# The factors that join two attention parts: 32 rows sent through DRAM, instead of a spread and 16 transposes on the chip

## The chip, the cores and the metric

The kernel runs on one core of one Trainium2 chip. The time is in device microseconds (us), as the median of several runs of the whole program. A core has a matrix engine (PE, with its weight load shown as PEld), a vector engine (DVE), a scalar engine (ACT), a general engine (POOL), and a queue (SP) that here issues all the transfers (DMAs) between DRAM and the on-chip memory. Each engine, and SP, takes its instructions strictly in order; an instruction that must wait for another engine or for a transfer holds up everything behind it on the same engine.

## The reference

A decoder trunk of two layers, 1024 tokens by 1024 features, in float32. What matters here, cut from the reference:

```python
for l in range(DEPTH):
    h = rmsnorm(x, norm1[l])
    proj = h @ w_in[l]
    qa, ka, va, qb, kb, vb, gate_pre = jnp.split(proj, splits, axis=-1)
    o_a = dilated_mixture(hd4(qa, DSW_HEADS), hd4(ka, DSW_HEADS), hd4(va, DSW_HEADS))
    o_b = stick_breaking_attention(hd4(qb, SB_HEADS), hd4(kb, SB_HEADS), hd4(vb, SB_HEADS))
    g_a, g_b = (sigmoid(gate_pre + b_gate[l]) in two halves)
    merged = g_a * (o_a @ w_br[l, :OUT_A]) + g_b * (o_b @ w_br[l, OUT_A:])
    x = x + merged @ w_o[l]
    h2 = rmsnorm(x, norm2[l])
    ...
# dilated_mixture: three groups of four heads, each with its own window and dilation;
# per head slot the groups' outputs are mixed by their softmax denominators:
alpha = jax.nn.softmax(jnp.stack(lses, axis=0), axis=0)
o = jnp.sum(alpha[..., None] * jnp.stack(outs, axis=0), axis=0)
```

The kernel holds the mixture of the two nearer groups as one unnormalised sum `on` with its own maximum and denominator (`sn`), and the widest group as `ot` with `st1`. Mixing the two needs, for every token and head, two factors: one for `on` and one for `ot`. The features of a head lie on 64 partitions and the tokens run along the free axis, so a factor has to stand in all 64 partitions of its head. The statistics come with the tokens on partitions. Bringing the factors from the one layout to the other is what the change is about.

## The kernel before

Every float32 product is made of three matmuls: both operands are split into a high part and a remainder (ACT casts `w_hi`, `hh`; DVE subtracts to `w_lo`, POOL to `hl`), and high*high, high*low and low*high are summed in PSUM. L182, L183 and L184 are the three matmuls of the plain form (`product`), L1017 to L1019 those of the large input projection.

A layer runs in these stages. The input projection (dense work, L1017 to L1019) is interleaved on PE with attention: a list of attention items is worked off between the dense steps. The last 16 items are the far ones, eight for each of two pairs of heads (`pr` 0 and 1). After the last far item of a pair, `join` mixes `on` and `ot`. `dense.at(n, f)` makes `f` run n dense steps later; the two halves of a join run 2 and 4 steps after the last item.

Then come the branch products, 16 items i = 0 to 15, each a half of the tokens by 128 output features. An item has a product with the attention outputs `oh_a` (called a_i here) and one with `oh_b` (b_i), two times three matmuls each, multiplied by gates `gin` on DVE (L1433), summed into `mrg` (m_i, L1438), and cast and split by ACT (`hh`, L1398) and POOL (`hl`, L1399). The order on PE is b0 b1 b2 a0 a1 a2 a3 b3 a4 b4, and so on to a15 b15. After item i the program loads the gates of item i + 3 (`gate_in`, L1373: 512 KB into one of the four `p4` buffers, which it shares with `fx`), and after i = 1, 5 and 9 the branch weights that items 4, 8 and 12 begin with (`branch_in`, L1391: `br_raw`, 512 KB, split into `br_w` by two ACT casts and two DVE subtractions). The second, third and fourth of these loads in a layer are called br_raw #2, #3 and #4. Then the output projection `o_ps` follows with weights `w_raw`, and the feed-forward part.

PE's order is written out by hand: for the whole program, PE takes its instructions in the order of the code. DVE, ACT, POOL and SP are ordered by a list scheduler, which goes by dependences, priorities and its own estimate of when each is ready. So a change of a few instructions can move others on those four.

The join before, in words: `factors(pr)` computes the two factors as `sf`, a 128 x 16 tile each (L959 to L968, after the last score of the pair). ACT spreads them with four copies (L974) into two tiles `fx`, 64 equal columns a head. The join then makes, for each half, eight transposes of 128 x 128 on PE (L988) into two PSUM banks `j_ps`, and three DVE operations: `jn = ot * j_ps` (L991), `on = on * j_ps` (L992), `on = on + jn` (L993). After them `on` is cast to `oh_a`.

Of the kernel before, what the change touches and what calls it, by code (L numbers as in the profile page):

```python
# [7 lines left out]
F32 = mybir.dt.float32  # L8
# [4 lines left out]
ALU = mybir.AluOpType  # L13
# [3 lines left out]
P = 128  # L17
T = 1024
D = 1024
KD = D // P  # L20
HF = 512
# [12 lines left out]
PT = 6  # L34
# [17 lines left out]
X_AT = (3, 5, 7, 9)  # L52
AHEAD = 200
JOIN = 4


def f32(ap):
# [4 lines left out]
def trunk_kernel(ctx, tc, x, norm1, w_in, b_gate, w_br, w_o, norm2, w_up, conv_w, conv_b, w_down, norm_f, out, depth=None, probe=None):  # L62
    nc = tc.nc
    act, dve, pe, pool = nc.scalar, nc.vector, nc.tensor, nc.gpsimd
# [4 lines left out]
    sb = ctx.enter_context(tc.tile_pool(name="sb", bufs=1))  # L69
    ps = ctx.enter_context(tc.tile_pool(name="ps", bufs=2, space=PSUM))  # L70
    dr = ctx.enter_context(tc.tile_pool(name="dr", bufs=1, space=DRAM))


    ident = cp.tile([P, P], F32, name="ident")
# [46 lines left out]
    sq = [dr.tile([2, 2, 64, T], F32, name=f"sq{i}") for i in range(4)]  # L121
    sv = [dr.tile([P, n, KD, P], F32, name=f"sv{n}") for n in (4, 2, 2)]
    dn = [dr.tile([4, T], F32, name=f"dn{i}") for i in range(2)]

    def bank(tag, name):
        return ps.tile([P, 512], F32, tag=tag, name=name)

    def small(name, dtype=F32):
        return sb.tile([P, 512], dtype, tag="pt", bufs=PT, name=name)
# [431 lines left out]
    R = {}  # L561
# [83 lines left out]
    def scores(o, qt, ql, k):  # L645
        pe.matmul(o, qt, k, start=True, stop=False, skip_group_check=True)
        pe.matmul(o, ql, k, start=False, stop=True, skip_group_check=True)
# [235 lines left out]
    def far_item(dense, pr, s, r, share):  # L883
        i = 8 * pr + 4 * s + r
# [7 lines left out]
        def score():  # L892
            if r == 0:
                bias = share["bias"] = sb.tile([P, 2, 256], F32, tag="bias", name="bias1")
                dve.tensor_scalar(bias[:, 0, :], base0, 4.0 * SLOPES[4 + slot], None, ALU.mult)
                dve.tensor_scalar(bias[:, 1, :], base2, 4.0 * SLOPES[8 + slot], None, ALU.mult)
            bias = share["bias"]
            pt = shared["p"] = sb.tile([P, T], F32, tag="p4", bufs=4, name="p1")
            z0, z1 = bank("s", "z10"), bank("s", "z11")
            t = R["kq", i % 2]  # L900
            for g in range(2):
                scores(z0[:, P * g : P * g + P], t[:, g, 1, 0:P], t[:, g, 2, 0:P], t[:, g, 0, 0:P])
            for g in range(2):
                scores(z1[:, 256 * g : 256 * g + 256], t[:, g, 1, P:256], t[:, g, 2, P:256], t[:, g, 0, :])
            dense.scored = i + 1
            if (s, r) == (1, 0):
                near_stats(pr)
            for n in range(2):
                flat = pt[:, 256:768] if n else pt[:, 0:256]
                if n:  # L910
                    zz, pp, bb = z1, flat, bias.rearrange("p g c -> p (g c)")
                else:
                    zz, pp, bb = z0[:, 0:256].rearrange("p (g c) -> p g c", g=2), flat.rearrange("p (g c) -> p g c", g=2), bias[:, :, P:256]
                nm = st[:, 0, s, n, r : r + 1]
                with tc.high_priority(offset=AHEAD):
                    LAST["red"] = dve.tensor_tensor_reduce(pp, zz, bb, 1.0, 3e38, ALU.add, ALU.min, nm).ins.name
                    act.activation(flat, flat, AF.Exp, bias=nm, scale=-1.0, accum_out=st[:, 1, s, n, r : r + 1])
            if (s, r) == (1, 3):
                factors(pr)

        def turn(g):
            pt = shared["p"]
# [25 lines left out]
    def near_stats(pr):  # L948
        sn = R["sn", pr] = sb.tile([P, 2, 2, 2, 4], F32, tag="sn", bufs=1, name="sn")
        nc.sync.dma_start(sn.rearrange("j a s n r -> j (a s) n r"), tok_view(dn[pr]))  # L950

    def factors(pr):

        sn, st = R["sn", pr], R["st1", pr]
        nat, far_ = (t.rearrange("j a s n r -> j a (s n r)") for t in (sn, st))
        w = sb.tile([P, 6, 16], F32, tag="sw", bufs=1, name="sw")
        f = R["f", pr] = sb.tile([P, 2, 2, 2, 4], F32, tag="sf", bufs=1, name="sf")
        ff = f.rearrange("j a s n r -> j a (s n r)")
        dve.tensor_tensor(w[:, 0, :], nat[:, 0, :], far_[:, 0, :], ALU.min)  # L959
        dve.tensor_tensor(w[:, 1, :], w[:, 0, :], nat[:, 0, :], ALU.subtract)  # L960
        dve.tensor_tensor(w[:, 2, :], w[:, 0, :], far_[:, 0, :], ALU.subtract)
        act.activation(w[:, 1:3, :], w[:, 1:3, :], AF.Exp)
        dve.tensor_tensor(w[:, 3, :], w[:, 1, :], nat[:, 1, :], ALU.mult)
        dve.tensor_tensor(w[:, 4, :], w[:, 2, :], far_[:, 1, :], ALU.mult)
        dve.tensor_tensor(w[:, 3, :], w[:, 3, :], w[:, 4, :], ALU.add)
        dve.reciprocal(w[:, 5, :], w[:, 3, :])
        dve.tensor_tensor(ff[:, 0, :], w[:, 1, :], w[:, 5, :], ALU.mult)
        dve.tensor_tensor(ff[:, 1, :], w[:, 2, :], w[:, 5, :], ALU.mult)  # L968

        R["fx", pr] = []  # L970
        for a in range(2):
            fx = sb.tile([P, 2, 4, 2, 64], F32, tag="p4", bufs=4, name="fx")
            for s in range(2):
                act.copy(fx[:, :, :, s, :], f[:, a, s, :, :].unsqueeze(3).to_broadcast([P, 2, 4, 64]))  # L974
            R["fx", pr].append(fx.rearrange("p n r s c -> p n r (s c)"))

    def join(dense, pr):

        fx, on, ot = R["fx", pr], R["on"], R["ot", pr]
        mine = on[:, pr, :].rearrange("p (n j r) -> p n r j", n=2, r=4)  # L980
        other = ot.rearrange("p (r n j) -> p n r j", r=4, n=2)

        def half_of(n):
            spread = []
            for a in range(2):
                o = bank("to"[a], "j_ps")
                for r in range(4):
                    pe.transpose(o[:, r * P : (r + 1) * P], fx[a][:, n, r, :], ident)  # L988
                spread.append(o.rearrange("p (r j) -> p r j", r=4))
            t = small("jn").rearrange("p (r j) -> p r j", r=4)  # L990
            dve.tensor_tensor(t, other[:, n], spread[1], ALU.mult)  # L991
            dve.tensor_tensor(mine[:, n], mine[:, n], spread[0], ALU.mult)  # L992
            dve.tensor_tensor(mine[:, n], mine[:, n], t, ALU.add)  # L993

        dense.at(2, lambda: half_of(0))
        dense.at(JOIN, lambda: half_of(1))

# [1174 lines left out]
```

## Time and profile before

| | |
|---|---|
| median of 3 runs | 2615.86 us (2615.82 to 2617.07) |
| the profiled execution | 2618.04 us, of which the span from first to last instruction 2616.1 us |
| mean granted TensorE clock | 0.999 |
| PE busy | 2606.0 us (100% of the span) |
| PE weight load, DVE, ACT, POOL busy | 84%, 80%, 52%, 4% |
| chain of work that ended last | PE 96%, everything else 1% or less each |
| DMA | 468.22 MB, mean 179 GB/s, HBM read 303.23 MB and written 162.59 MB |

A matmul row shows a start and a duration. Matmuls overlap: the distance between the starts of two that follow each other is what a matmul takes of PE's time, not the duration in the row. A row with xN is a group of N; a remark in square brackets tells how long the engine stood idle before and what ended that. A DMA row on SP (SPq) shows when the transfer was issued; the time to its landing is given apart.

### The profile page before, as it was taken

Reading aid. Unit: us, or ns where it says so; the run is one execution under the profiler, and the core shown is the slowest. Engines: PE = TensorE matmul, PEld = TensorE weight load, DVE = VectorE, ACT = ScalarE, POOL = GpSimd, SP = SyncE. Lnnn points to the kernel's source line nnn. Section 1 sums busy time; section 2 is a strip of 40 time slices with the busy share of each in tenths; the row PEclk is TensorE's granted clock in tenths of the full one; section 3 lists DMA queues with packets and bytes.
Section 4 is the critical chain, followed back from the end, with each engine's and each line's share of the span. In section 5 each row is a group of like instructions: output and inputs, shape, how many; then the busy total and the mean of one; then the engine's idle time right before and its main releaser. Section 6 shows DMA issues by size and latency. Waiting matters only on the chain.

```text
span 2616.1 us, 36210 instructions
## 1 busy us (share of the span) xinstructions
PE 2606.0 (100%) x12736; PEld 2185.2 (84%) x12736; DVE 2089.5 (80%) x3484; ACT 1357.6 (52%) x2533; POOL 102.2 (4%) x135
## 2 busy tenths in 40 slices
PE   9999999999999999999999999999999999999999
PEld 8888888888888888888888888888888888888888
DVE  7877777795988888897677788777869888889965
ACT  6555666574554555422445555666645555544225
POOL 3000000020000000000000000000300000000000
PEclk9999999999999999999999999999999999999999
DMA  7434578873344444688344436787633344447962
GB/s 254 151 120 132 161 207 217 214 247 93 93 145 153 145 164 142 234 326 317 145 145 147 125 128 180 203 231 210 207 99 119 125 161 146 150 164 260 347 238 111
DMA packets 400418, 468.22 MB, mean 179 GB/s; under 512 B 24308, under 2 KB 315500, under 8 KB 398444
## 3 DMA queue, kind: packets, MB, share of 16 engines
q1 hardware_dynamic: 400220, 465.90, 55.3%
q8 instruction: 101, 1.65, 0.3%
q14 instruction: 81, 0.66, 0.1%
q10 hardware_dynamic: 16, 0.00, 0.0%
HBM read 303.23 MB, written 162.59 MB: 178 GB/s over the span
## 4 chain that ended last, share of the span: by engine, by line
PE 96%; DVE 1%; DMA 1%; ACT 1%; issue 1%; SPq 0%; POOL 0%; DVEq 0%; ACTq 0%
PE u_a L1019 6%; PE u_a L1018 6%; PE u_a L1017 6%; PE d_ps L1780 5%; PE d_ps L1781 5%; PE d_ps L1782 5%; PE i_a L1017 5%; PE i_a L1019 5%; PE i_a L1018 5%; PE u_c L1017 3%; PE u_c L1019 3%; PE u_c L1018 3%; PE i_c L1017 3%; PE i_c L1019 3%; PE i_c L1018 3%; PE o_ps L183 2%
## 5 line engine op out<-in xcount | busy, mean ns | idle before, releaser
L141 ACT CAST w_hi<-up_a 128x512 fp32r<-128x512 f32 x280 | 173.9, 622 | 276.5 <-DVE up_a L1634 120.5
L148 DVE TENSOR_TENSOR w_lo<-up_a,w_hi 128x512 fp32r<-128x512 f32 x280 | 189.3, 688 | 83.6 <-ACT w_hi L141 83.6
L141 ACT CAST w_hi<-in_a 128x512 fp32r<-128x512 f32 x252 | 156.2, 622 | 162.9 <-PE i_c L1018 38.0
L148 DVE TENSOR_TENSOR w_lo<-in_a,w_hi 128x512 fp32r<-128x512 f32 x252 | 172.7, 687 | 75.8 <-ACT w_hi L141 67.0
L1788 DVE TENSOR_TENSOR x<-x,d_ps 128x512 f32<-128x512 f32 (+1 forms) x228 | 153.4, 674 | 65.0 <-PE d_ps L1782 61.6
L1780 PE MATMUL d_ps<-gd_in,w_hi 128*128 128x512 f32 (+1 forms) x340 | 130.0, 382 | 0.0
L1782 PE MATMUL d_ps<-gd_in,w_lo 128*128 128x512 f32 (+1 forms) x340 | 129.8, 382 | 0.0
L1781 PE MATMUL d_ps<-gd_in,w_hi 128*128 128x512 f32 (+1 forms) x340 | 129.7, 382 | 0.0
L1019 PE MATMUL u_a<-hh,w_lo 128*128 128x512 f32 x320 | 124.5, 389 | 0.0
L1018 PE MATMUL u_a<-hl,w_hi 128*128 128x512 f32 x320 | 124.5, 389 | 0.0
L1017 PE MATMUL u_a<-hh,w_hi 128*128 128x512 f32 x320 | 124.5, 389 | 0.0
L1017 PE MATMUL u_a<-t_hi,w_hi 128*128 128x512 f32 x320 | 124.5, 389 | 0.0
L1019 PE MATMUL u_a<-t_hi,w_lo 128*128 128x512 f32 x320 | 124.5, 389 | 0.0
L1018 PE MATMUL u_a<-t_lo,w_hi 128*128 128x512 f32 x320 | 124.5, 389 | 0.0
L1017 PE MATMUL i_a<-hh,w_hi 128*128 128x512 f32 x288 | 119.2, 414 | 0.0
L1017 PE MATMUL i_a<-t_hi,w_hi 128*128 128x512 f32 x288 | 118.3, 411 | 0.0
L1780 PE MATMUL d_ps<-gd_in,wd 128*128 128x512 f32 (+1 forms) x292 | 113.9, 390 | 0.0
L1019 PE MATMUL i_a<-hh,w_lo 128*128 128x512 f32 x288 | 113.2, 393 | 0.0
L1019 PE MATMUL i_a<-t_hi,w_lo 128*128 128x512 f32 x288 | 113.0, 393 | 0.0
L1018 PE MATMUL i_a<-t_lo,w_hi 128*128 128x512 f32 x288 | 112.9, 392 | 0.0
L1018 PE MATMUL i_a<-hl,w_hi 128*128 128x512 f32 x288 | 112.8, 392 | 0.0
L1782 PE MATMUL d_ps<-gd_in,wd 128*128 128x512 f32 (+1 forms) x292 | 112.8, 386 | 0.0
(380 smaller groups left out, 7834.9 us busy)
## 6 DMA issues: line engine op xcount, KB each, us to landing
gd<-g SPq DMA_DIRECT2D x154, 512.0 KB, 3.3
gd_in<-gd SPq DMA_DIRECT2D x154, 512.0 KB, 5.9
up_a<-in_w_up_dram SPq DMA_DIRECT2D x80, 512.0 KB, 5.2
in_a<-in_w_in_dram SPq DMA_DIRECT2D x72, 512.0 KB, 5.3
wd_raw<-in_w_down_dram SPq DMA_DIRECT2D x22, 1024.0 KB, 11.2
gin<-gs SPq DMA_DIRECT2D x32, 512.0 KB, 3.8
w_raw<-in_w_o_dram SPq DMA_DIRECT2D x64, 256.0 KB, 2.9
gs<-u SPq DMA_DIRECT2D x48, 256.0 KB, 3.2
```

The lines of the kernel that those rows point to most:

```text
L141: one = act.copy(hi, src)
L148: two = dve.tensor_tensor(lo, src, f32(hi), ALU.subtract)
L183: pe.matmul(o, lh, rl, start=False, stop=False, skip_group_check=share)
L1017: pe.matmul(o, w[0][:, c], rh, start=(first and i == 0), stop=False, skip_group_check=True)
L1018: pe.matmul(o, w[0][:, c], rl, start=False, stop=False, skip_group_check=True)
L1019: pe.matmul(o, w[1][:, c], rh, start=False, stop=(last and i == 3), skip_group_check=True)
L1780: pe.matmul(o[:, sub], wh[:, c], gh[:, sub], start=(i == 0 and k in (0, 4, 5)), stop=False, skip_group_check=True)
L1781: pe.matmul(o[:, sub], wh[:, c], gl[:, sub], start=False, stop=False, skip_group_check=True)
L1782: pe.matmul(o[:, sub], wl[:, c], gh[:, sub], start=False, stop=(i == m - 1), skip_group_check=True)
L1788: dve.tensor_tensor(x, x, o[:, sub], ALU.add)
```

## The change

`factors` computes the same factors as one tile `sf` of 128 x 32. Three dense steps later (`SEND`), `send` transposes it once on PE into 32 rows (`f_t`, L975), ACT copies them out of PSUM (`f_r`, L978), and SP writes them to a DRAM tensor `fd` of 16 KB (L979). Four more DMAs read `fd` back (L984): each takes one row of 1024 factors and writes it to 64 partitions, 256 KB on the chip. Two tiles `fx` of 128 x 1024 result, in the layout of `on` and `ot`. The join is left with three DVE operations a half, all on operands in on-chip memory: `ot = ot * fx` (L997), `on = on * fx` (L998), `on = on + ot` (L999). This happens four times, for two pairs in two layers. Lines behind the change move by up to six (L916 becomes L918, L1373 becomes L1379, L1391 becomes L1397, L1433 becomes L1439, L1438 becomes L1444).

```diff
--- before.py
+++ after.py
@@ -52,6 +52,7 @@
 X_AT = (3, 5, 7, 9)
 AHEAD = 200
 JOIN = 4
+SEND = 3
 
 
 def f32(ap):
@@ -121,6 +122,7 @@
     sq = [dr.tile([2, 2, 64, T], F32, name=f"sq{i}") for i in range(4)]
     sv = [dr.tile([P, n, KD, P], F32, name=f"sv{n}") for n in (4, 2, 2)]
     dn = [dr.tile([4, T], F32, name=f"dn{i}") for i in range(2)]
+    fd = [dr.tile([4, T], F32, name=f"fd{i}") for i in range(2)]
 
     def bank(tag, name):
         return ps.tile([P, 512], F32, tag=tag, name=name)
@@ -916,7 +918,7 @@
                     LAST["red"] = dve.tensor_tensor_reduce(pp, zz, bb, 1.0, 3e38, ALU.add, ALU.min, nm).ins.name
                     act.activation(flat, flat, AF.Exp, bias=nm, scale=-1.0, accum_out=st[:, 1, s, n, r : r + 1])
             if (s, r) == (1, 3):
-                factors(pr)
+                factors(dense, pr)
 
         def turn(g):
             pt = shared["p"]
@@ -949,13 +951,12 @@
         sn = R["sn", pr] = sb.tile([P, 2, 2, 2, 4], F32, tag="sn", bufs=1, name="sn")
         nc.sync.dma_start(sn.rearrange("j a s n r -> j (a s) n r"), tok_view(dn[pr]))
 
-    def factors(pr):
+    def factors(dense, pr):
 
         sn, st = R["sn", pr], R["st1", pr]
         nat, far_ = (t.rearrange("j a s n r -> j a (s n r)") for t in (sn, st))
         w = sb.tile([P, 6, 16], F32, tag="sw", bufs=1, name="sw")
-        f = R["f", pr] = sb.tile([P, 2, 2, 2, 4], F32, tag="sf", bufs=1, name="sf")
-        ff = f.rearrange("j a s n r -> j a (s n r)")
+        f = sb.tile([P, 2, 2, 8], F32, tag="sf", bufs=1, name="sf")
         dve.tensor_tensor(w[:, 0, :], nat[:, 0, :], far_[:, 0, :], ALU.min)
         dve.tensor_tensor(w[:, 1, :], w[:, 0, :], nat[:, 0, :], ALU.subtract)
         dve.tensor_tensor(w[:, 2, :], w[:, 0, :], far_[:, 0, :], ALU.subtract)
@@ -964,33 +965,38 @@
         dve.tensor_tensor(w[:, 4, :], w[:, 2, :], far_[:, 1, :], ALU.mult)
         dve.tensor_tensor(w[:, 3, :], w[:, 3, :], w[:, 4, :], ALU.add)
         dve.reciprocal(w[:, 5, :], w[:, 3, :])
-        dve.tensor_tensor(ff[:, 0, :], w[:, 1, :], w[:, 5, :], ALU.mult)
-        dve.tensor_tensor(ff[:, 1, :], w[:, 2, :], w[:, 5, :], ALU.mult)
-
-        R["fx", pr] = []
-        for a in range(2):
-            fx = sb.tile([P, 2, 4, 2, 64], F32, tag="p4", bufs=4, name="fx")
-            for s in range(2):
-                act.copy(fx[:, :, :, s, :], f[:, a, s, :, :].unsqueeze(3).to_broadcast([P, 2, 4, 64]))
-            R["fx", pr].append(fx.rearrange("p n r s c -> p n r (s c)"))
+        dve.tensor_tensor(f[:, 0].rearrange("j s k -> j (s k)"), w[:, 1, :], w[:, 5, :], ALU.mult)
+        one, two = (w[:, k, :].rearrange("j (s n r) -> j s n r", s=2, n=2) for k in (2, 5))
+        for x in range(2):
+            dve.tensor_tensor(f[:, 1, x].rearrange("j (r n) -> j n r", n=2), one[:, x], two[:, x], ALU.mult)
+
+        def send():
+            tp = bank("t", "f_t")
+            pe.transpose(tp[0:32, 0:P], f.rearrange("j a s k -> j (a s k)"), ident)
+            row = sb.tile([32, P], F32, tag="pt", bufs=PT, name="f_r")
+            with tc.high_priority(offset=AHEAD):
+                act.copy(row, tp[0:32, 0:P])
+            nc.sync.dma_start(fd[pr].rearrange("c (k p) -> (c k) p", p=P), row)
+            R["fx", pr] = []
+            for a in range(2):
+                fx = sb.tile([P, T], F32, tag="p4", bufs=4, name="fx")
+                for x in range(2):
+                    nc.sync.dma_start(fx[64 * x : 64 * x + 64, :], fd[pr][2 * a + x : 2 * a + x + 1, :].to_broadcast([64, T]))
+                R["fx", pr].append(fx)
+
+        dense.at(SEND, send)
 
     def join(dense, pr):
 
-        fx, on, ot = R["fx", pr], R["on"], R["ot", pr]
-        mine = on[:, pr, :].rearrange("p (n j r) -> p n r j", n=2, r=4)
-        other = ot.rearrange("p (r n j) -> p n r j", r=4, n=2)
+        on, ot = R["on"], R["ot", pr]
 
         def half_of(n):
-            spread = []
-            for a in range(2):
-                o = bank("to"[a], "j_ps")
-                for r in range(4):
-                    pe.transpose(o[:, r * P : (r + 1) * P], fx[a][:, n, r, :], ident)
-                spread.append(o.rearrange("p (r j) -> p r j", r=4))
-            t = small("jn").rearrange("p (r j) -> p r j", r=4)
-            dve.tensor_tensor(t, other[:, n], spread[1], ALU.mult)
-            dve.tensor_tensor(mine[:, n], mine[:, n], spread[0], ALU.mult)
-            dve.tensor_tensor(mine[:, n], mine[:, n], t, ALU.add)
+            first, second = R["fx", pr]
+            mine, far = on[:, pr, n * HF : (n + 1) * HF], ot.rearrange("p (r n j) -> p n r j", r=4, n=2)[:, n]
+            mine = mine.rearrange("p (j r) -> p r j", r=4)
+            dve.tensor_tensor(far, far, second.rearrange("p (r n j) -> p n r j", r=4, n=2)[:, n], ALU.mult)
+            dve.tensor_tensor(mine, mine, first[:, n * HF : (n + 1) * HF].rearrange("p (r j) -> p r j", r=4), ALU.mult)
+            dve.tensor_tensor(mine, mine, far, ALU.add)
 
         dense.at(2, lambda: half_of(0))
         dense.at(JOIN, lambda: half_of(1))
```

On PE, the 64 transposes of L988 go and four of L975 come. The scheduler also orders other engines anew. Three places:

DVE, first layer, from the last factor of pair 0 on (`p`, `st` <- `z`, `bias` is the reduction of a far item's scores; `p1l` the remainder of its predecessor's transposed probabilities). Before:

```order
L968 TENSOR_TENSOR sf<-sw 128x16
L1145 TENSOR_TENSOR in_a<-in_a 128x512
L916 ISA p_5190,st_5186<-z_5191,bias_5187 128x256
L916 ISA st_5186 128x1
L148 TENSOR_TENSOR w_lo<-in_a,w_hi 128x512
L916 ISA p_5190,st_5186<-z_5192,bias_5187 128x512
L916 ISA st_5186 128x1
L1195 TENSOR_TENSOR u<-u,i_b 128x512
L148 TENSOR_TENSOR p1l<-t_5216,p1h 128x384
L1148 TENSOR_TENSOR in_a<-in_a 128x512
L148 TENSOR_TENSOR w_lo<-in_a,w_hi 128x512
L148 TENSOR_TENSOR p1l<-t_5240,p1h 128x384
```

And after the change:

```order
L971 TENSOR_TENSOR sf<-sw 128x2x4 x2
L1151 TENSOR_TENSOR in_a<-in_a 128x512
L150 TENSOR_TENSOR w_lo<-in_a,w_hi 128x512
L1201 TENSOR_TENSOR u<-u,i_b 128x512
L150 TENSOR_TENSOR p1l<-t_5224,p1h 128x384
L150 TENSOR_TENSOR p1l<-t_5248,p1h 128x384
L918 ISA p_5198,st_5194<-z_5199,bias_5195 128x256
L918 ISA st_5194 128x1
L918 ISA p_5198,st_5194<-z_5200,bias_5195 128x512
L918 ISA st_5194 128x1
L1154 TENSOR_TENSOR in_a<-in_a 128x512
L918 ISA p_5271,st_5194<-z_5272,bias_5195 128x256
```

The reductions of `z_5199` and `z_5200` (before: `z_5191` and `z_5192`) now stand behind two subtractions to `p1l`, of which they stood ahead.

ACT, first layer, at the end of the attention (`gin<-gin,bg` is a sigmoid of the gates, `oh_a<-on` the cast behind the join). Before:

```order
L1379 ACT_TABLE_LOAD
L1379 ACTIVATE gin<-gin,bg 128x512 x2
L141 CAST oh_b<-ob_in 128x512 x2
L661 COPY fold<-o_5814 64x512
L141 CAST oh_a<-on 128x512 x2
L1379 ACTIVATE gin<-gin,bg 128x512 x2
L141 CAST br_w<-br_raw 128x512 x2
L141 CAST oh_a<-on 128x512
L1204 COPY last<-i_a 128x512
L141 CAST oh_a<-on 128x512
```

And after:

```order
L143 CAST br_w<-br_raw 128x512 x2
L1210 COPY last<-i_a 128x512
L143 CAST oh_a<-on 128x512
L1385 ACT_TABLE_LOAD
L1385 ACTIVATE gin<-gin,bg 128x512 x2
L143 CAST oh_a<-on 128x512
L1385 ACTIVATE gin<-gin,bg 128x512 x6
L1404 CAST hh_5947<-mrg 128x512 x2
L1404 CAST hh_5965<-mrg 128x512
```

The load of the sigmoid's table and all the sigmoids now stand behind the first cast that needs the second pair's join.

SP, first layer, in the branch products (`gin` in the order of the items; the first row shown is the gates of item 3 before and of item 5 after). Before:

```order
L1373 DMA gin_6015<-gs_88 128x1024
L1391 DMA br_raw_6135<-in_w_br_dram 128x4x256
L465 DMA x1_6215<-xs1_87 128x2048
L1373 DMA gin_6031<-gs_88 128x1024
L1373 DMA gin_6054<-gs_88 128x1024
L1373 DMA gin_6080<-gs_88 128x1024
L1391 DMA br_raw_6242<-in_w_br_dram 128x4x256
L1373 DMA gin_6104<-gs_88 128x1024
L1373 DMA gin_6130<-gs_88 128x1024
L163 DMA w_raw_6320<-in_w_o_dram 128x4x128
```

And after:

```order
L1379 DMA gin_6024<-gs_88 128x1024
L1379 DMA gin_6050<-gs_88 128x1024
L1379 DMA gin_6074<-gs_88 128x1024
L1379 DMA gin_6100<-gs_88 128x1024
L1397 DMA br_raw_6105<-in_w_br_dram 128x4x256
L1379 DMA gin_6131<-gs_88 128x1024
L467 DMA x1_6135<-xs1_87 128x2048
L1379 DMA gin_6157<-gs_88 128x1024
L1379 DMA gin_6181<-gs_88 128x1024
L467 DMA x1_6185<-xs1_87 128x2048
L1379 DMA gin_6207<-gs_88 128x1024
L1397 DMA br_raw_6212<-in_w_br_dram 128x4x256
```

br_raw #3 (`br_raw_6135` before, `br_raw_6105` after) stood behind the gates of item 3 and now stands behind those of item 8; br_raw #4 stood behind those of item 6, now behind those of item 12. The loads of `w_raw` start behind the last `gin` instead of between them. The second layer is ordered in the same way.

## The prediction

> **What bounds the kernel now.** I read the page first: span, engines, and the chain that ended last.
>
> ```profile
> span 2616.1 us, 36210 instructions
> PE 2606.0 (100%) x12736; PEld 2185.2 (84%) x12736; DVE 2089.5 (80%) x3484; ACT 1357.6 (52%) x2533; POOL 102.2 (4%) x135
> PE 96%; DVE 1%; DMA 1%; ACT 1%; issue 1%; SPq 0%; POOL 0%; DVEq 0%; ACTq 0%
> ```
>
> PE is never free. So an instruction less on PE is worth what it takes of PE's time, a microsecond of PE waiting costs a microsecond, and work on another engine is worth nothing unless PE waits for it. Two questions follow: what do the removed transposes take, and does PE wait for anything new? Four joins are touched, two in each layer; I count for one layer and double.
>
> **The transposes that go.** The timeline of PE around joins in the first layer:
>
> ```profile
> 485.17 1.03 PE L988 MATMUL j_ps<-ident,fx 128*128 128x128 f32 x8
> 485.96 0.30 PE L646 MATMUL z<-t_kq 128*128 128x128 f32 x1
> ...
> 538.76 0.47 PE L1017 MATMUL i_a<-hh,w_hi 128*128 128x512 f32 x1
> 539.07 0.39 PE L1018 MATMUL i_a<-hl,w_hi 128*128 128x512 f32 x1
> ```
>
> Eight transposes are busy for 1.03 us, but the next matmul starts 485.96 - 485.17 = 0.79 after them, since they overlap. Behind another group the first dense matmul keeps PE for 539.07 - 538.76 = 0.31 instead of the 0.23 at which this kernel's 512-wide matmuls follow each other (18 of them from 557.93 to 562.01 in rows below, 0.227 each); 0.08 more. A half join is thus worth 0.87, four in a layer **-3.5**.
>
> **What comes on PE.** A transpose of the same shape exists for the near statistics (`st_t`). The other rows are PE and DVE where the first pair's new transpose will stand.
>
> ```profile
> L841 PE MATMUL st_t<-ident,st x4: 272/272/273, 372.2 to 1711.0; 128*32 128x128 f32 x4
> ...
> 471.13 0.17 DVE L968 TENSOR_TENSOR sf<-sw 128x16 f32<-128x16 f32 x1
> ...
> 471.44 0.22 PE L646 MATMUL z<-t_kq 128*128 128x128 f32 x1
> ```
>
> Pipelined, it takes about what an eighth of the group above takes, 0.1; alone, up to its 0.27. It goes in at 471.44, just after the last DVE operation of the factors, which starts at 471.13 and, with the new second half of it, ends about 471.4: nothing to spare. It also takes a bank of tag `t`, for which the attention's own transposes then wait a little. I take 0.3 for each of two, **+0.6** (0.2 to 0.9).
>
> **The far item behind the first join.** The order puts two reductions of a far item behind a `p1l` that is ready late, and their exponentials behind a copy. Rows of PE, DVE and ACT there:
>
> ```profile
> 476.18 0.36 PE L934 MATMUL o<-p1h,slots 128*128 128x256 f32 x1
> 476.67 0.39 PE L934 MATMUL o<-p1l,slots 128*128 128x256 f32 x1
> ...
> 479.43 0.27 PE L924 MATMUL t<-ident,p 128*128 128x128 f32 x1
> ...
> 481.14 0.28 PE L934 MATMUL o<-p1h,slots 128*128 128x256 f32 x1
> 481.26 0.28 PE L934 MATMUL o<-p1l,slots 128*128 128x256 f32 x1
> ...
> 478.50 0.55 DVE L148 TENSOR_TENSOR p1l<-t,p1h 128x384 fp32r<-128x384 f32 x1
> ...
> 480.30 0.42 DVE L916 CUSTOM_DVE_ANT_1 p<-z,bias 128x256 f32<-128x256 f32 x1
> ...
> 481.25 0.08 DVE L916 DVE_READ_ACCUMULATOR2_ANT st<- 128x1 f32 x1
> ...
> 474.84 0.73 ACT L917 ACTIVATE p<-p,st 128x512 f32<-128x512 f32 x1 [0.86 <-DVE st L916]
> ```
>
> That `p1l` runs from 478.50, or from 478.25 if it goes first, so to about 478.8. A pair of reductions takes 481.25 + 0.08 - 480.30 = 1.03, which is 479.8; the second exponential 0.73, which is 480.5. PE wants the result in the transposes of 479.43: it waits 1.1. Against it, PE's wait of 0.37 at 476.18 (0.49 to the next matmul, where the same two stand 0.12 apart at 481.14) goes, since DVE is free earlier. Net **+0.7** (0 to 0.9).
>
> **Spread, factors and join off PE.** Removed on ACT are four copies a pair; DVE has three operations a half as before. No DVE operation of the join is on PE's path except through `oh_a`. What is new is a chain through DRAM. The nearest transfers: `dn<-st_r` writes the same 32 rows, `kv<-sk` brings 256 KB to 64 partitions as `fx` does.
>
> ```profile
> kv<-sk SPq DMA_DIRECT2D x16, 256.0 KB, 4.6
> dn<-st_r SPq DMA_DIRECT2D x4, 16.0 KB, 3.4
> ...
> 524.06 0.62 ACT L974 COPY fx<-sf 128x512 f32<-128x512 f32 x1
> ...
> 536.98 0.68 DVE L991 TENSOR_TENSOR jn<-ot,j_ps 128x512 f32<-128x512 f32 x1
> ...
> 540.87 0.62 ACT L141 CAST oh_a<-on 128x512 fp32r<-128x512 f32 x1 [3.33 <-DVE on L993]
> ```
>
> For the second pair the factors are done when the spread began before, 524.06; three dense steps, transpose and copy bring the write to about 526. Then 3.4, four issues of some 0.45 (a DMA's issue is 0.41 in rows below), and 4.6: about 536, a microsecond before the 536.98 at which the join began. So the join is not later, and its cover is that one microsecond. But the table load and all sigmoids now stand behind the `oh_a` of 540.87, where two items' sigmoids were done before; the first gates come just when PE wants their banks freed. **+0.4** (0, if the join runs ahead; 3, if both landings take 1.5 longer).
>
> **The branch weights.** This is the large term. SP takes its list in order, and br_raw #3 now stands behind the gates of item 8, which wait for the buffer that m4 frees on DVE. Rows of SP, DVE (both layers' m4) and PE:
>
> ```profile
> 543.01 0.41 SPq L1391 DMA_DIRECT2D br_raw<-in_w_br_dram  x1
> ...
> 556.02 3.93 SPq L1373 DMA_DIRECT2D gin<-gs  x2
> ...
> 1834.62 0.42 SPq L1391 DMA_DIRECT2D br_raw<-in_w_br_dram  x1
> ...
> 1846.78 2.85 SPq L1373 DMA_DIRECT2D gin<-gs  x2
> ...
> 557.82 1.78 DVE L1438 TENSOR_TENSOR mrg<-gin 128x512 f32<-128x512 f32 x1
> ...
> 1848.58 0.69 DVE L1438 TENSOR_TENSOR mrg<-gin 128x512 f32<-128x512 f32 x1
> ...
> 557.93 0.39 PE L182 MATMUL br_ps<-oh_b,br_w 128*128 128x512 f32 x1
> ...
> 562.01 0.39 PE L182 MATMUL br_ps<-oh_a,br_w 128*128 128x512 f32 x1
> ...
> 1853.61 0.39 PE L182 MATMUL br_ps<-oh_a,br_w 128*128 128x512 f32 x1
> ```
>
> Before, #3 was issued at 543.01, 19 us ahead of a8 (562.01), its first user. The gates of item 8 are the second of the pair at 556.02 and go at about 559.6, right at the end of m4 (557.82 + 1.78); in the second layer at 1849.3 (1848.58 + 0.69). a8 starts 2.4 and 4.3 us after m4's end. What does the load need?
>
> ```profile
> DMA to landing us min/median/max: 4.4/6.1/6.5
> ...
> DMA to landing us min/median/max: 3.3/3.8/6.0
> ...
> L141 ACT CAST br_w<-br_raw x16: 602/616/647, 522.3 to 1859.1; 128x512 fp32r<-128x512 f32 x16
> ...
> L148 DVE TENSOR_TENSOR br_w<-br_raw,br_w x16: 676/680/1749, 524.4 to 1861.1; 128x512 fp32r<-128x512 f32 x16
> ```
>
> The first line is `br_raw`, the second `gin`, of the same 512 KB. From m4's end: the gates' issue and its own, 0.45; landing, 6.1 as the load at 1834.62, which had a `gin` just ahead too; two casts and a subtraction (the half that a8 needs is cast second), 2.0, less the 0.45 that PE can spend on the two matmuls that don't need the remainder: 8.1 in all. PE waits 8.1 - 4.3 = 3.8 or 8.1 - 2.4 = 5.7 us; **+4.7** (2.1 with the 4.4 landing and the longer interval, 6.1 with 6.5 and the shorter).
>
> br_raw #4 stands behind the gates of item 12 and thus m8. After PE has waited at a8, m8 follows on its heels: a8 and b8 take 12 matmuls of 0.227, 2.7; a multiply and a merge 1.3 to 1.9, then 8.1: 12.1 to 12.7 after a8's start. a12 comes 48 matmuls, 10.9, after it. PE waits again, **+1.5** (0 to 2.4).
>
> The loads of `w_raw` start later but PE arrives later too: nothing. And a wait of the output projection goes:
>
> ```profile
> 588.53 0.39 PE L182 MATMUL o_ps<-hh,w_hi 128*128 128x512 f32 x1
> 589.38 0.50 PE L183 MATMUL o_ps<-hl,w_hi 128*128 128x512 f32 x1 [0.46 <-POOL hl L1399]
> ```
>
> 0.85 from one to the next instead of 0.23: while PE waits for weights, DVE and POOL catch up, **-0.6** (0 at worst).
>
> **The sum.** For a layer -3.5 + 0.6 + 0.7 + 0.4 + 4.7 + 1.5 - 0.6 = +3.8, for two +7.6. The profiled execution took 2618.04 (span 2616.1), so 2625.6 by it; it is 2.2 above the median of the runs, 2615.86, which becomes 2623.5. With all lower ends: 2 x (-3.5 + 0.2 + 0 + 0 + 2.1 + 0 - 0.6) = -3.6, 2612.3; with all upper ends 2 x (-3.5 + 0.9 + 0.9 + 3 + 6.1 + 2.4) = +19.6, 2635.5.
>
> **Rivals.** A change within 0.2%, 5.2 us, can't be told from none here.
>
> *The loads are quick.* If br_raw lands in the 3.3 of the quickest `gin` instead of 6.1, #3 costs 4.7 - 2.8 = 1.9 and #4 nothing: -0.5 for a layer, 2614.9, no change. For it: when #3 goes out at the new place, only one `gin` is under way. Against it: none of the `br_raw` seen took under 4.4. [...]
>
> *The merges run ahead* (the other side). The price of #3 rests on the interval from m4 to a8. If DVE's merges came 3.8 us earlier against PE than in the second layer before, the weights would be there: nothing for #3 and #4, nothing for the gates: -3.5 + 0.6 + 0.7 - 0.6 = -2.8, two layers -5.6, 2610.3, faster. For it: m4's 1.78 is stretched beyond the 0.69 of its twin, and the join waits for no PSUM any more. Against it: the sigmoids start later than before, so merges are more likely late. It decides at 8.1 us between m4's end and a8.
>
> *The factors land late.* If write and read each take 1.5 longer than the medians I used, the join, `oh_a` and the first gates come 3 later than in the forecast, and PE stands at a0; m4 and a8 move together, so the other terms stay: +2 x 3 = 6 more than the forecast, 2629.5, slower.
>
> **How the numbers follow.** The forecast (weights late twice, 2618.5 to 2630) gets 0.57, quick loads 0.16, merges ahead 0.12, late factors 0.15. Faster by over 0.2% (under 2610.6) is the merges' case with a small part lost to its upper half, 0.11; no change takes the quick loads and the low end of the forecast's own range up to 2621.1, 0.26; slower has the rest, 0.63. The likeliest time is 2623.5. The range cuts half of the two outer cases: 2612 to 2630.
>
> **What would show it.** In the profile after: no L988; PE's waits name `t` behind an exponential of ACT about 480 (1.1), and `br_ps` behind `br_w` at a8 (4 to 6 in each layer) and at a12 (0 to 2.4), with br_raw #3 issued straight after a `gin` about 557. The join's first DVE operation shows whether it waited for `fx`. I am wrong if br_raw #3 lands before PE has finished b7, or if PE waits at a0 for `oh_a` by microseconds.

## The result

The changed kernel takes 2635.0 us (median of 6 runs, 2634.0 to 2637.14) against 2616.03 for the kernel before on the same chips (6 runs): slower, ratio 1.0071 with a 95% interval of 1.0058 to 1.0084. The forecast, 2623.5, had the sign and the place, but the loss is 19 us instead of 7.6, and the time lies outside the range.

The profiled execution took 2634.51 us, span 2632.7, mean clock 0.997 (0.999 before). The page's span, engines and chain, and then what PE waited for (us in total, times, the longest):

```profile
span 2632.7 us, 36096 instructions
PE 2608.0 (99%) x12676; PEld 2181.3 (83%) x12676; DVE 2084.2 (79%) x3488; ACT 1351.4 (51%) x2521; POOL 101.7 (4%) x135
PE 91%; DVE 4%; DMA 2%; ACT 2%; issue 1%; POOL 0%; SPq 0%; DVEq 0%; ACTq 0%
```

```profile
PE br_ps L184 <- ACT br_w L143: 11.9, 4, 3.3
PE br_ps L186 <- DVE br_w L150: 1.5, 2, 0.7
PE u_c L1023 <- ACT u L1659: 1.1, 2, 0.6
PE t L927 <- ACT p L919: 0.8, 2, 0.4
```

PE has 60 instructions less, yet is busy 2 us longer (2608.0 against 2606.0), and the waits, 13.4 of them for branch weights, don't add up to the 16.6 by which the span grew on top of the 7 us of transposes saved. So something made PE's own work longer. To find where, the program is cut at two places of each layer: the first branch product and the first output product. The rows of the first layer on PE, before and after the change:

```profile
540.23 0.40 PE L182 MATMUL br_ps<-oh_b,br_w 128*128 128x512 f32 x1
...
583.77 0.39 PE L182 MATMUL o_ps<-hh,w_hi 128*128 128x512 f32 x1
```

```profile
537.37 0.39 PE L184 MATMUL br_ps<-oh_b,br_w 128*128 128x512 f32 x1
...
591.84 0.39 PE L184 MATMUL o_ps<-hh,w_hi 128*128 128x512 f32 x1
```

| stretch of PE, us | before | after | kernel of the last experiment |
|---|---|---|---|
| start to the first branch product | 540.23 | 537.37 | 537.13 |
| branch products, first layer | 43.54 | 54.47 | 43.52 |
| to the first branch product of the second layer | 1248.06 | 1246.03 | 1246.56 |
| branch products, second layer | 43.54 | 54.45 | 43.52 |

Outside the branch products the change gains, 2.9 and 2.0 us, and 0.3 behind the last of them. Inside, each layer loses 10.9, and that is the whole result. The rows of PE at the first of the two places, where a8 begins:

```profile
558.90 0.39 PE L186 MATMUL br_ps<-oh_b,br_w 128*128 128x512 f32 x1
561.94 0.50 PE L184 MATMUL br_ps<-oh_a,br_w 128*128 128x512 f32 x1 [2.65 <-ACT br_w L143]
562.28 0.40 PE L185 MATMUL br_ps<-ol_a,br_w 128*128 128x512 f32 x1
562.75 0.79 PE L186 MATMUL br_ps<-oh_a,br_w 128*128 128x512 f32 x1
563.34 0.63 PE L184 MATMUL br_ps<-oh_a,br_w 128*128 128x512 f32 x1
563.77 0.63 PE L185 MATMUL br_ps<-ol_a,br_w 128*128 128x512 f32 x1
...
566.18 0.40 PE L185 MATMUL br_ps<-ol_b,br_w 128*128 128x512 f32 x1
566.41 0.39 PE L186 MATMUL br_ps<-oh_b,br_w 128*128 128x512 f32 x1
```

First the wait that was forecast: 3.04 from start to start, 2.8 more than the usual 0.227. Then something that was not: the matmuls behind it start 0.43 apart, half as fast, until 566.18, though none of them waits for anything. The granted clock in stretches of 4 us says why (PE busy, its instructions, PEclk, DMA share, GB/s):

```profile
554.00:558.00 4.00, 4.00 (x20) 1.00 0.75 268
558.00:562.00 4.00, 1.35 (x7) 1.00 1.06 394
562.00:566.00 4.00, 3.93 (x10) 0.57 0.78 288
566.00:570.00 4.00, 4.00 (x19) 1.00 0.96 376
```

Behind this wait PE ran at about half its clock for some 4 us (0.57 granted from 562 to 566, matmuls 0.43 apart up to 566.18). From 558.90 to 566.18 there are 11 matmuls, 2.5 us by the usual spacing, and they take 7.28: 4.8 lost, 2.8 by waiting and 2.0 by the clock. At a12 it is 6.15 (574.58 to 583.22), 4.2 and 2.0; in the second layer 4.7 and 6.15. Together 21.8, of which 14 are waits and about 8 the clock.

The waits have the cause that was forecast, in part. SP, ACT and DVE of the changed kernel in the first layer:

```profile
547.57 7.89 SPq L1379 DMA_DIRECT2D gin<-gs  x5
555.52 0.43 SPq L1397 DMA_DIRECT2D br_raw<-in_w_br_dram  x1
...
568.36 0.32 SPq L1379 DMA_DIRECT2D gin<-gs  x1
568.73 0.43 SPq L1397 DMA_DIRECT2D br_raw<-in_w_br_dram  x1
...
560.75 1.14 ACT L143 CAST br_w<-br_raw 128x512 fp32r<-128x512 f32 x2 [0.18 <-DMA br_raw<-in_w_br_dram]
...
576.59 0.62 ACT L1404 CAST hh<-mrg 128x512 fp32r<-128x512 f32 x1 [0.82 <-DVE mrg L1444]
577.12 1.13 ACT L143 CAST br_w<-br_raw 128x512 fp32r<-128x512 f32 x2
...
553.38 1.74 DVE L1444 TENSOR_TENSOR mrg<-gin 128x512 f32<-128x512 f32 x1
...
575.87 0.69 DVE L1444 TENSOR_TENSOR mrg<-gin 128x512 f32<-128x512 f32 x1
```

The first row of DVE is m4, which ends at 555.12. br_raw #3 goes out at 555.52, right behind the gates of item 8, and its cast waits for its landing at 560.7, 5.2 later. br_raw #4 goes out at 568.73. But its cast, at 577.12, waits for no transfer: ACT stands before it at the cast of m11, which needs m11 of 575.87, and that needs b11, the product just ahead of a12 on PE. So in this profile it is ACT's order that makes PE stand still there, from the end of b11 through a multiply, a merge and three casts. When br_raw #4 landed isn't known. With the longest landing known of a `br_raw` in this profile, 7.3 us, it was there at 576.0, an estimate; then ACT's order cost at least 1.1 of the 3.5 us, and more if it landed sooner.

### The profile page after: what moved, and what is told of

It is laid out like the page before. It is cut to its first block, busy times and chain, and to the rows that moved or that the text cites. A ratio compares the mean times of both kernels' runs of the same rounds, so it can differ in the third digit from the quotient of the medians.

```text
span 2632.7 us, 36096 instructions
## 1 busy us (share of the span) xinstructions
PE 2608.0 (99%) x12676; PEld 2181.3 (83%) x12676; DVE 2084.2 (79%) x3488; ACT 1351.4 (51%) x2521; POOL 101.7 (4%) x135
## 3 DMA queue, kind: packets, MB, share of 16 engines
q8 instruction: 100, 1.64, 0.3%
## 4 chain that ended last, share of the span: by engine, by line
PE 91%; DVE 4%; DMA 2%; ACT 2%; issue 1%; POOL 0%; SPq 0%; DVEq 0%; ACTq 0%
PE u_a L1024 5%; PE u_a L1025 5%; PE u_a L1023 5%; PE d_ps L1786 5%; PE d_ps L1788 5%; PE d_ps L1787 5%; PE i_a L1023 5%; PE i_a L1025 5%; PE i_a L1024 5%; PE u_c L1023 3%; PE u_c L1024 3%; PE u_c L1025 3%; PE i_c L1023 2%; PE i_c L1025 2%; PE i_c L1024 2%; PE o_ps L184 2%
## 5 line engine op out<-in xcount | busy, mean ns | idle before, releaser
L1786 PE MATMUL d_ps<-gd_in,wd 128*128 128x512 f32 (+1 forms) x292 | 113.9, 390 | 0.0
L1788 PE MATMUL d_ps<-gd_in,wd 128*128 128x512 f32 (+1 forms) x292 | 112.8, 386 | 0.0
L1787 PE MATMUL d_ps<-gd_in,wd 128*128 128x512 f32 (+1 forms) x292 | 112.7, 386 | 0.0
## 6 DMA issues: line engine op xcount, KB each, us to landing
wd_raw<-in_w_down_dram SPq DMA_DIRECT2D x22, 1024.0 KB, 12.7
```

Source lines behind the costliest of these rows:

```text
L1786: pe.matmul(o[:, sub], wh[:, c], gh[:, sub], start=(i == 0 and k in (0, 4, 5)), stop=False, skip_group_check=True)
L1787: pe.matmul(o[:, sub], wh[:, c], gl[:, sub], start=False, stop=False, skip_group_check=True)
L1788: pe.matmul(o[:, sub], wl[:, c], gh[:, sub], start=False, stop=(i == m - 1), skip_group_check=True)
```

## The experiments

Theory A: the whole loss comes from the place of br_raw #3 and #4 on SP (and of their casts behind it), by PE's waits and the half clock after them. Rival B: the route through DRAM itself costs, by late joins and crowded transfers. Rival C: the slow matmuls wait for operands; the clock has nothing to do with it. Every ratio is to runs of the kernel before on the same chip.

**What a wait costs.** Into the output projections of the kernel before, 16 holds of graded length:

```diff
+    def hold(k):
...
+        o, d = bank("o", "hold"), small("hold_d")
+        pe.transpose(o[:, 0:P], ident, ident)
+        with tc.high_priority(offset=AHEAD):
+            act.copy(d[:, 0:P], o[:, 0:P])
+            for j in range(k - 1):
+                act.copy(d[:, (j + 1) % 2 * P : (j + 1) % 2 * P + P], d[:, j % 2 * P : j % 2 * P + P])
+        pe.transpose(o[:, P : 2 * P], d[:, (k - 1) % 2 * P : (k - 1) % 2 * P + P], ident)
...
+        hold(HOLD[l].get(8 * n + e, 0))
```

> The kernel before, with 16 waits of graded length put into the output projections of both layers: a transpose on PE, then a chain of 1 to 24 small copies on ACT, then a transpose that needs the last copy. It measures by itself what a wait of PE costs beyond its length. Theory A: waits under about 1.5 us are followed by matmuls at 0.23 us; those of 3 us and more by some 4 us at 0.43 us, 2 us lost each, whatever the length; between them it may be either. Rival C: no matmul behind a wait is slow, since here its operands lie ready.

PE's rows about two of the holds, and the clock in the 4 us behind each:

```profile
619.88 0.27 PE L1286 MATMUL hold<-ident 128*128 128x128 f32 x1
623.02 0.33 PE L1291 MATMUL hold<-ident,hold_d 128*128 128x128 f32 x1 [2.87 <-ACT hold_d L1290]
623.11 0.48 PE L183 MATMUL o_ps<-hh,w_hi 128*128 128x512 f32 x1
623.42 0.39 PE L184 MATMUL o_ps<-hl,w_hi 128*128 128x512 f32 x1
...
705.22 0.27 PE L1286 MATMUL hold<-ident 128*128 128x128 f32 x1
712.97 0.47 PE L1291 MATMUL hold<-ident,hold_d 128*128 128x128 f32 x1 [7.47 <-ACT hold_d L1290]
713.10 0.77 PE L183 MATMUL o_ps<-hh,w_hi 128*128 128x512 f32 x1
713.67 0.63 PE L184 MATMUL o_ps<-hl,w_hi 128*128 128x512 f32 x1
```

```profile
623.00:627.00 4.00, 3.98 (x18) 1.00 0.11 34
713.00:717.00 4.00, 4.00 (x10) 0.50 0.00 0
```

For all 16, the gap from start to start, and what the matmuls behind it lost above 0.227 each:

| gaps, us | lost behind them, us |
|---|---|
| 2.48, 2.81, 3.14, 3.83 | 0.1 each |
| 3.47, 3.65, 3.74, 4.06 | 1.65, 1.66, 1.69, 1.69 |
| 4.16 to 9.72 (eight) | 1.7 to 2.7 |

Behind the twelve that lost 1.65 or more, some 3.4 to 5.6 us ran at half clock, and the holds of 4.16 to 9.72 cost at most about one microsecond more than those of the second row. No hold came out shorter than 2.48, so what was expected of waits under 1.5 was not tried here. Rival C falls: these operands lay ready. In the second row the half clock of three of the four began 1.1 to 1.3 us after PE had started again, not with the end of the wait.

**PE kept busy.** In the changed kernel, extra matmuls just ahead of a8 and a12:

```diff
+                    old = wb if i else None
...
+            if (i, ab) in ((8, 0), (12, 0)):
+                for _ in range({8: 12, 12: 15}[i]):
+                    pe.matmul(o, old[0][0][:, 0, ec], xh[:, 0, sl], start=True, stop=True, skip_group_check=True)
```

> The changed kernel, with 12 and 15 extra matmuls of 128x512 put on PE just ahead of a8 and a12 in each layer, into the bank that the next product overwrites; they fill PE's waits there (2.8 and 3.5 us) and change nothing else. Theory A (after a wait of some 3 us PE runs at half clock for about 3.9 us, which costs 2.0 us each of the four times): the granted clock stays 1.00, matmuls behind the waits follow at 0.23 us, and the time falls by about 8, to 2627. Rival C (the slow matmuls behind the waits wait for operands, or PE is simply late): the spacing of 0.43 stays and the time is 2635 or, with the extra matmuls on top, up to 2647.

2629.55 us (4 runs, ratio to before 1.0049, 1.0035 to 1.0063): 5.5 less than the changed kernel by doing more. The extra matmuls ahead of a8 run from 562.84 to 565.56, and PE still waits once more behind them, from 565.79 to 567.71, for a remainder; but the clock stays up, as the same stretches as above show:

```profile
562.84 2.88 PE L1439 MATMUL br_ps<-oh_a,br_w 128*128 128x512 f32 x12
...
567.71 0.50 PE L186 MATMUL br_ps<-oh_a,br_w 128*128 128x512 f32 x1 [1.53 <-DVE br_w L150]
```

```profile
562.00:566.00 4.00, 4.00 (x19) 1.00 1.06 401
566.00:570.00 4.00, 2.47 (x11) 1.00 0.61 246
```

The branch products take 51.5 and 49.7 instead of 54.5 twice, 7.7 less together, near the 8 that were expected. Against it stand new waits of 2.9 and 2.3 us in that profile, at the far item's scores behind the first joins, for keys that landed up to 8.0 us after their issue. Transfers are crowded there: the changed kernel, without these two waits, has a DMA share of 1.03 to 1.07 from 474 to 486.

**The late loads alone.** The kernel before, with the two loads held behind the gates of items 8 and 12:

```diff
+                LAST["gin"] = nc.sync.dma_start(gt, gs[e, n]).ins.name
...
+                one = nc.sync.dma_start(raw, w_br[l].rearrange("(k p) n -> p k n", p=P)[:, :, e * P : (e + 2) * P])
+                if i >= 8:
+                    tc.add_manual_dep(one.ins, LAST["gin"], NO_SYNC, reason="behind")
```

> The kernel before, join and factors untouched, with br_raw #3 and #4 held on SP behind the gates of items 8 and 12. Theory A: the waits and the half clock appear without the change, 10 to 11 us a layer: 2636 to 2639. Rival B: without the route through DRAM the loads are quick enough or the waits small: 2616 to 2624.

2626.77 us (ratio 1.0041, 1.0026 to 1.0057): slower without any of the change's transposes or transfers, but 10 us instead of 19, and between the two times that were expected. PE's waits here:

```profile
PE br_ps L182 <- ACT br_w L141: 4.6, 2, 3.3
PE br_ps L184 <- DVE br_w L148: 1.9, 2, 1.7
```

Its branch products take 46.1 and 49.5. Merges and casts stand otherwise than in the changed kernel, so the waits are 6.5 in all instead of 13.4, and no half clock followed any of them in the profiled execution, even one of 3.68 (the clock was 1.00 in each stretch of 4 us from 1855 to 1875). Two of the other three executions took 3 us longer, at a mean clock of 0.998 instead of 1.000; in these it may have. The place on SP is enough for a loss; its size hangs on what else is in line.

**Only the first of the two mended.** Higher priority for the casts of the branch weights:

```diff
-                    split(*parts_[q], raw[:, 2 * q : 2 * q + 2, :])
+                    with tc.high_priority(offset=AHEAD):
+                        split(*parts_[q], raw[:, 2 * q : 2 * q + 2, :])
```

> The changed kernel with the higher priority on the casts and subtractions of the branch weights only. SP then has br_raw #3 behind the gates of item 4, but #4 still behind those of item 12; on ACT the casts of #4 come one cast of hh sooner, ahead of that of m11, which needs the product just before a12. It undoes the first of the two waits alone, and parts the second into transfer and ACT's order. Theory A: nothing at a8 (2.8 us and 2.0 of half clock in each layer gone, -9.5); at a12, if ACT's order made the wait of 4.2, it falls to 2 or less and no half clock follows: 2614 to 2620; if the transfer made it, it stays about 4 with its half clock: about 2625.

2632.3 us, ratio 1.0062 (1.0049 to 1.0076), above both times that were expected.

```profile
PE br_ps L184 <- ACT br_w L143: 7.8, 2, 3.9
PE f_t L975 <- DVE sf L971: 5.0, 2, 2.5
```

The wait at a8 is gone; that at a12 is 3.9 in both layers, with half clock behind it (in the first layer the matmuls start 0.43 apart from 577.64 to 581.91). ACT there, in the first layer:

```profile
574.11 0.62 ACT L1405 CAST hh<-mrg 128x512 fp32r<-128x512 f32 x1 [1.94 <-DVE mrg L1445]
574.64 1.33 ACT L1385 ACTIVATE gin<-gin,bg 128x512 f32<-128x512 f32 x2
575.87 1.12 ACT L143 CAST br_w<-br_raw 128x512 fp32r<-128x512 f32 x2
576.90 0.61 ACT L1405 CAST hh<-mrg 128x512 fp32r<-128x512 f32 x1
```

The two casts moved ahead of one cast of a merge, m11's, and now stand behind the one before it, which waits 1.94 for m10, and behind two sigmoids. They wait for no transfer here either. So the repair exchanged one place in ACT's order for another as bad; how early the weights of br_raw #4 had landed, and what PE would wait with ACT free, the rows don't tell. And the scheduler made a new wait: PE at a new transpose of each layer, 2.5.

**The loads put first.** Higher priority for the loads of the branch weights (the first two lines), then for the output weights too, then with the transpose sent sooner:

```diff
+                with tc.high_priority(offset=AHEAD):
+                    nc.sync.dma_start(raw, w_br[l].rearrange("(k p) n -> p k n", p=P)[:, :, e * P : (e + 2) * P])
...
+        with tc.high_priority(offset=AHEAD):
+            w = weights(w_o[l][:, e * P : (e + 1) * P], P)
...
-SEND = 3
+SEND = 1
```

> The changed kernel, with one thing undone: the loads of the branch weights are given a higher priority, so that br_raw #3 and #4 stand on SP ahead of the gates of items 4 to 8. Theory A (the whole loss comes from the place of these two loads on SP: PE waits for them and then runs at half clock): no wait of PE on br_w, clock 0.999, and what is left is -7 for 64 transposes, +1.8 for the far item's transposes behind the first join and +0.5 for the new transposes: about 2611. Rival B (the loss belongs to the route through DRAM itself: join, sigmoids and gates later, transfers in each other's way): the waits move to other places and the time stays above 2625.

> The changed kernel with the higher priority on the loads of the branch weights (as in the first run of this study, 2621.0) and on the output weights too. On SP the first six loads of the output weights come between the gates instead of behind the last. Theory A: the waits of 2.2 and 2.3 us at the first output product and the slow matmuls behind the second go, -4 to -7: 2614 to 2617, with what is left of the change's own gain covered by the waits about the first joins. Rival B: it stays at 2621.

> As the run with branch and output weights first, and the new transpose and the transfers of the factors one dense step after the last score instead of three. The factors come about a microsecond sooner to the join, the transpose stands closer to the DVE work it waits for. If late factors still cost (DVE waited 1.3 us for fx in the changed kernel) it is faster, 2611 to 2615; if the transpose on PE now waits for DVE (its operand was ready 0.05 us before it was wanted), slower by that wait, 0.7 us a time, about 2617 to 2620.

Measured: 2621.0 (ratio 1.0018, 1.0009 to 1.0027), 2630.34 (1.0051, 1.0039 to 1.0064) and 2622.93 (1.0026, 1.0016 to 1.0036). None waits for branch weights any more. The largest waits of PE in each, in this order:

```profile
PE o_ps L184 <- ACT w_hi L143: 4.5, 3, 2.2
```

```profile
PE o_ps L184 <- DVE gin L1441: 8.5, 2, 4.4
```

```profile
PE f_t L975 <- DVE sf L971: 7.2, 4, 2.0
```

In the first, 14 of the 19 us are back, and now the output weights, which still stand behind all the gates, come late. In the second they were put ahead of gates, have only two buffers, and wait on SP for these; the last gates wait behind them, and PE for the gates, 4.4 twice, with half clock behind both (the mean clock of this execution is 0.997). My expectation there was wrong in sign. In the third, where the output weights stand singly between the gates on SP, no wait is left in the branch products (43.7 and 43.5), but the transpose comes before DVE is done, 1.8 each of four times, where 0.7 was expected.

**The factors from another queue.** Write and reads of the factors issued by POOL; the other two runs also ask for the branch weights sooner, or give them priority.

```diff
-            nc.sync.dma_start(fd[pr].rearrange("c (k p) -> (c k) p", p=P), row)
+            nc.gpsimd.dma_start(fd[pr].rearrange("c (k p) -> (c k) p", p=P), row)
...
-                    nc.sync.dma_start(fx[64 * x : 64 * x + 64, :], fd[pr][2 * a + x : 2 * a + x + 1, :].to_broadcast([64, T]))
+                    nc.gpsimd.dma_start(fx[64 * x : 64 * x + 64, :], fd[pr][2 * a + x : 2 * a + x + 1, :].to_broadcast([64, T]))
```

> The changed kernel with the write of the factors and the four reads issued from POOL's queue instead of SP's; nothing else is edited. SP's list then comes out with br_raw #3 behind the gates of item 3 again, #4 behind those of item 11 (6 before the change, 12 with it), and the output weights between the last gates. Theory A (the loss is in what SP's order does to the loads of weights): no wait at a8, at a12 up to 2 us, no wait for the output weights, 2610 to 2617. Rival B (the route through DRAM itself costs, by late joins and crowded transfers): above 2621. Rival D (POOL issues and starts its transfers so much later that fx comes late): PE waits at a0, above 2625.

> As the run with POOL's queue, and the program asks for br_raw #3 and #4 one and two items sooner (after items 4 and 7 instead of 5 and 9); on SP they come behind the gates of items 3 and 7. Theory A: no wait for branch weights at all, what is left of the change is -7.0 for the transposes, +0.5 for the new ones and up to +1.8 behind the first joins: 2609 to 2612, faster than the kernel before. Rival B: above 2616.

> As the run with POOL's queue, and the loads of the branch weights have the higher priority of the run that put them first: both come ahead of the gates of item 3, and the first output weights ahead of the gates of item 13. Theory A: as in the last run, 2609 to 2612; it differs from the first priority run (2621.0) only by the queue of the factors and the place of the output weights, and so measures these two. Rival B: as that run, about 2621.

2632.28, 2632.05 and 2632.73: 1.0063 (1.0050 to 1.0075) for the first, the others within 0.0002 of it. Rival D, that `fx` comes late by POOL's queue, is what happened. In the first of them, who waited for `fx` and how long its reads took:

```profile
  DVE on L998: 12.7, 4
```

```profile
DMA to landing us min/median/max: 3.6/5.1/9.0
```

DVE waited for `fx` 12.7 us in four joins, where it waited 1.3 in the changed kernel. Everything behind the join on DVE is late with it, and PE waits in many places, at `p1h` (5.0 us), at the projection's sums (2.7) and at `ol_a` (2.0). The microsecond of cover that the forecast gave the factors was not there: with SP's queue, too, the second pair's join waited for them, 0.6 and 0.7.

**Only the two loads taken off SP.** The factors stay on SP; br_raw #3 and #4 are issued by POOL, which in the changed kernel stood idle for 128.8 us up to the first `hl` at 548.34:

```diff
-                nc.sync.dma_start(raw, w_br[l].rearrange("(k p) n -> p k n", p=P)[:, :, e * P : (e + 2) * P])
+                (nc.gpsimd if i >= 8 else nc.sync).dma_start(raw, w_br[l].rearrange("(k p) n -> p k n", p=P)[:, :, e * P : (e + 2) * P])
```

> The changed kernel with br_raw #3 and #4 alone issued from POOL's queue, which stands idle until the first hl; the factors stay on SP. They no longer stand behind any gates, and ACT's casts of them come early, too. Theory A: no wait at a8 and a12, no half clock there, which gives back 21.8 of the profiled execution; left are the transposes' -7, some 1.8 about the first joins, 1.0 of the wait at u_c, and 0 to 4 a layer if the output weights, still behind nearly all the gates, come late as in the first priority run: 2612 to 2619. Rival B (the crowded transfers and late joins of the route through DRAM are the cost): waits at a0 or before it, above 2624.

2614.06 us (11 runs, 2612.56 to 2617.76), ratio 0.9993 with 0.9984 to 1.0002: the whole loss is gone, by one line. In the first layer the two loads go out at 542.2 and 547.9 instead of 555.5 and 568.7. The profiled execution's span is 2610.8, 5.3 under that of the kernel before, though it is the quickest of the 11 and that one was 2 us over its median; its branch products take 43.52 twice, and apart from the program's first wait PE's largest is

```profile
PE u_c L1023 <- ACT u L1659: 1.1, 1, 1.1
```

Rival B falls as the cause: route, transfers and late sigmoids are all still there. The gain of this version over the kernel before can't be told from none by the runs; its executions differ by 5 us where those of the kernel before differ by 2.4. Single waits of 1.6 to 2.7 us ahead of a far item's scores were seen in the profiles of five other variants (in the row `PE z L648`), and none in this one's; whether they come and go between executions and make this spread was not tried.

## Why the prediction was wrong

- *"A microsecond of PE waiting costs a microsecond."* This step failed. Waits of 2.7 to 3.5 us cost another 2.0 each through the clock, four times, 8 us; no term of the sum had it. The holds agree in the size, 1.65 to 2.7, and gaps of 2.95 and 3.04 in the changed kernel, and of 2.48 and 2.56 in a variant, were already enough. The two waits of 4.7 in the forecast fall among the holds of 4.16 to 9.72, which lost 1.7 to 2.7 each; with that twice the forecast would have been 2627 to 2629, an estimate from the holds.
- *br_raw #3, +4.7 a layer.* The mechanism holds, the size was too large: 2.8. m4 ended 4.0 us before PE wanted a8, where 2.4 and 4.3 had been taken; the load landed in 5.2 instead of 6.1, and a8 began 1.2 behind the landing instead of 1.55.
- *br_raw #4, +1.5 a layer.* 4.2. I counted only transfer and casts; ACT's order, with m11's cast ahead, was not looked at for this load. From m8's end to a12's start it was 10.0 instead of 8.1, and a wait of 0.7 for a remainder followed. The half clock at a8 delayed m8 and a12 alike and adds nothing to this wait. Together the two waits are 7.0 against 6.2 forecast: the sum of waits was nearly right, by two errors.
- *The transposes, -3.5 a layer, and the new ones, +0.3 each.* PE comes 2.9 sooner to the first branch product, with 0.9 still lost at the far item: this fits, but was not measured alone. Before two of the four new transposes the weight load stood idle for 0.3; PE itself lost under 0.1 by it (470.51 to 470.82 between two starts).
- *The far item behind the first join, +0.7 net.* As forecast: the waits at the transposes after 479 are 0.9 for 1.1, and the 0.37 at 476.18 is gone.
- *Factors and sigmoids, +0.4.* No wait of PE up to b7: 95 matmuls from 537.37 to 558.90 in 21.53, 0.227 each. The factors came about 534, the join waited 0.6 for them.
- *The wait of the output projection, -0.6 a layer.* Gone, but the kernel before had it in its first layer alone: -0.6 once.
- Not forecast: 1.0 more at `u_c`, where the feed-forward part begins.

For both layers: 2 x (-3.5 + 0.3 + 0.9 - 0.4 + 7.0 + 4.0 + 0.5) - 0.6 = 17.0, where the spans differ by 16.6; the -3.5 and the 0.3 in it are not measured alone. The medians differ by 2.4 more, because the profiled execution of the kernel before was 2 us over its median and that of the changed one 0.5 under. That all upper ends of the forecast sum to 2635.5, close to what was measured, is chance: they hold late gates and a larger #3, which did not come, and no clock.

None of the rivals is what happened. At a8 the landing of 5.2 lies between the 3.3 of the quick loads and the 6.1 of the forecast. The merges did not run ahead: m4 ended 4.0 and 3.9 us before a8 was wanted, and 8.1 were needed. DVE waited 0.6 for the factors, but PE did not stand at a0.

## What to carry to other kernels

Where PE is the bound, look in the new order of each in-order list, the DMA queue first, for what a moved transfer pushes behind a wait; here two loads of weights that nobody edited cost 21.8 us, three times the 7 that 64 transposes were estimated to give, and moving just these to an idle queue gave it all back (2614.06 us). Price a new PE wait by what it cost here beyond its length: another 1.7 to 2.7 us by the clock behind the holds of 4.06 us and more, up to 2.0 behind gaps of 2.48 to 3.83, nothing behind single ones under 1.9. A priority that mends one such place moves others: of eight repairs tried here, only the one that took the two loads out of the line altogether made no new wait elsewhere.

## What was not expected of the hardware

- PE at half clock: matmuls of 128x512 start 0.43 apart instead of 0.227 for 3.4 to 5.6 us; in these profiles after every gap of 4 us and more, after no single one under 1.9, and after some between them: 2.48 in a variant, 2.56 and 2.95 did, 2.48 in a hold, 2.89, 3.14 and 3.83 did not; 1.96 did with another of 0.69 right behind it. Two gaps of 1.64 one right after the other did.
- 12 to 15 useless matmuls in the gap kept the clock at 1.00 and saved about 4 us a layer, even where a further gap of 1.92 followed them.
- The same small transfers issued by POOL instead of SP landed in up to 9.0 us instead of 5.7 (medians 5.1 and 5.2), and cost DVE 12.7 us of waiting instead of 1.3; the two loads of 512 KB a layer that POOL issued in the last experiment, in the first layer 13 and 21 us earlier than SP had, left PE no wait for branch weights.
